# A planner that may give copies, casts and scalings to either of two engines, with other step order and buffer limits

## The chip, the core and the metric

The kernel runs on one core of one Trainium2 chip. A core has a matrix engine (TensorE, "PE" in the profile, with its weight loads as "PEld"), a vector engine (VectorE, DVE), a scalar engine (ScalarE, ACT), GpSimd (POOL) and SyncE (SP). Each engine works through its own queue of instructions in order. In this kernel SP issues nearly all DMAs, POOL issues the DMAs that add into a buffer, and the engines wait for each other through semaphores. The metric is the device time of one execution in microseconds, as the median of several runs.

## The reference, cut to what matters

The reference computes two layers of a decoder over 512 positions of width 1024, in float32. Each layer is a mixer, a gated feed-forward part with a short causal convolution, and a gated embedding part, each between two RMS norms:

```python
for i in range(DEPTH):                                   # DEPTH = 2
    h = rmsnorm(x, mix_pre_g[i]);  z = h @ w_in[i]       # 1024 x 3206
    out_a = spatial_gating(gelu(a_u), gelu(a_v), ...)    # 4 heads x 64
    out_b = silu(r_g) * norm(retention_chunkwise(rq, rk, rv))   # 6 heads x 64, rotary
    out_c = forgetting_attention(f_q, f_k, f_v, log_f)   # 6 heads x 64, softmax
    x = x + rmsnorm(concatenate([out_a, out_b, out_c]) @ w_o[i], mix_post_g[i])
    h = rmsnorm(x, ffn_pre_g[i])
    g = causal_conv3(h @ w_gate[i]) + conv_b[i]          # 1024 x 4096
    x = x + rmsnorm((gelu(g) * (h @ w_up[i])) @ w_down[i], ffn_post_g[i])
    gate = sigmoid(rmsnorm(x, ple_pre_g[i]) @ w_ple_gate[i])
    x = x + rmsnorm((p[i] @ w_ple_proj[i]) * gate, ple_post_g[i])
```

## The kernel before, in words

**Arithmetic.** A float32 product is made of three matmuls in the faster type `fp32r`: each operand is held as a rounded high part and the remainder, and high x high, high x low and low x high are summed (`mm3`). The helper `split` makes the two parts: a copy into an `fp32r` tile (the high part, a CAST on ACT in the version before) and a subtraction on DVE (the low part, a TENSOR_TENSOR). Every weight that arrives by DMA (`graw`, `traw`, `eraw`) passes through `split`. The gate and up projections are computed in pairs by a seven-product scheme (`seven`): sums of weights are formed (`wg`, `wsa`, `wsb`, `wu`: by adding DMAs from POOL and additions on DVE, `seven_weights`), and the products accumulate in three PSUM banks, `beta`, `alpha` and `gamma`. Between the products the running value of `beta` is copied out twice (`gs`), that of `gamma` once (`us`), and the final `beta` is scaled into `us`. Since PE goes on adding into the same bank, it must wait at each of these copies until the copy has read the bank; another bank's product of 12 matmuls lies between.

**Stages of a layer.** The mixer steps stand in the string `STEPS`: `u`, `v`, `F` and `H` are projections and sums, `f0` to `f2` and `r0` to `r2` are the seven-product projections of the attention and the retention pairs, `a0` to `a2` the attention itself (`fox_attend`: scores `sps`, exponential `pe`, division by its sum, transposes `tps`, copies `fet`), `c0` to `c2` the retention, `g`, `G`, `L`, `s` the gates. Then come the output product (`wo`), the embedding product (`eps`), the feed-forward part, and the gated embedding part. In the feed-forward part 32 blocks of gate and up projections run; from block 4 on each also carries a quarter of the down products (`dn`) of the blocks before it.

**What sets the order.** The program records all instructions first (class `Plan`, `record`) and then plans (`issue`): it goes through time with its own costs (`cost`, `HOP`), puts each instruction whose inputs are there on its engine, earliest recorded first, and thereby fixes each engine's queue. The queues are then in order on the chip. Buffers are taken while planning: `AHEAD` says, by kind of work ("mix", "wo", "dn" for the down weights and so on), how many recorded instructions ahead of the oldest unfinished one a buffer may be taken, and `SETS` says how many large buffers lie in each of two regions, X and W. All instructions are issued by one line, so that the profile shows nearly all under L452 (L480 in the changed kernel); rows are told apart by their tiles.

Of the kernel before, what the change touches and what calls it, by code (L numbers as in the profile page):

```python
# [36 lines left out]
P = 128  # L37
# [13 lines left out]
class Plan:  # L51
# [95 lines left out]

    @staticmethod
# [21 lines left out]
    def record(self, engine, fn, method, args, kw):  # L170
# [36 lines left out]
        self.ops.append((engine, fn, args, kw, deps, used, self.cost(engine, method, outs, ins, args, kw)))  # L207
# [44 lines left out]
    def issue(self):  # L252
        ops = self.ops
# [67 lines left out]
        def take(i, now):  # L321
# [13 lines left out]
            heapq.heappush(waiting[o[0]], (at, i, i))  # L335
# [57 lines left out]
        columns = {}  # L393
        now = 0.0
        while len(order) < n:
            progress = False
            for e in names:
                while waiting[e] and waiting[e][0][0] <= now:
                    _, pr, i = heapq.heappop(waiting[e])
                    heapq.heappush(ready[e], (pr, i))  # L400
                if ready[e] and free[e] <= now:
# [37 lines left out]
            for e in names:  # L439
                if ready[e]:  # L440
# [53 lines left out]
STEPS = "u F H f0 g f1 r0 a0 v a1 G L s r1 r2 c0 f2 c1 c2 a2"  # L494
# [37 lines left out]
def body(ctx, tc, a, out):  # L532
# [3 lines left out]
        ("DVE", nc.vector), ("ACT", nc.scalar), ("POOL", nc.gpsimd), ("PE", nc.tensor), ("SP", nc.sync)))  # L536

# [110 lines left out]
    def split(dst_hi, dst_lo, src):  # L648
        A.copy(dst_hi, src)
# [45 lines left out]
    class Mixed(Plain):  # L695
# [11 lines left out]
        def __call__(self, c, x, halves=range(2)):  # L707
# [9 lines left out]
            for kh in halves:  # L717
# [6 lines left out]
                A.copy(self.whole[kh][:, :, ts], ps)  # L724
# [135 lines left out]
    def seven(h, ws, gs, us, scale=1.0, between=None):  # L860
# [13 lines left out]
        A.copy(gs[:, t1], be)  # L874
# [3 lines left out]
        A.copy(gs[:, t2], be)  # L878
        product(ga, part(sa, 1), "hd", True, False)
        if scale == 1.0:  # L880
            A.copy(us[:, t2], ga)
        else:
            A.mul(us[:, t2], ga, -scale)
# [9 lines left out]
        A.mul(us[:, t1], be, -scale)  # L893
# [47 lines left out]
    def mixers(l, hT, uv, ready):  # L941
# [28 lines left out]
        def ret_values():  # L970
            tm_chunk_major(hT, tm_units(a["w_rv"][l], 384), 384, lambda c, ps: (V.tensor_copy if c % 2 else A.copy)(rv[:, c, :], ps[:, 0:384]))
# [42 lines left out]
        def fox_values():  # L1014
# [4 lines left out]
            def fv_done(c, ps):  # L1019
                A.copy(fv[:, c, :], ps[:, 0:384])  # L1020
# [45 lines left out]
        def fox_attend(p, tiles):  # L1066
# [4 lines left out]
            for c in range(NCH):  # L1071
# [5 lines left out]
                for s, ps in enumerate(pss):  # L1077
# [10 lines left out]
                    V.tensor_scalar(out=e[:, 0:n], in0=e[:, 0:n], scalar1=den, scalar2=None, op0=ALU.mult)  # L1088
# [3 lines left out]
                    (A.copy if c % 2 else V.tensor_copy)(et[s][:, 0:c + 1, c, :], tp[:, 0:n].rearrange("p (j t) -> p j t", t=P))  # L1092
# [11 lines left out]
        def ret_gate():  # L1104
            ps = bank("gps")
            fm_mm(ps, hT, fm_units(a["w_rg"][l]))
            A.copy(sg[:, 2, :], ps)
# [426 lines left out]
```

## Time and profile before

| | |
|---|---|
| median of 3 runs | 1566.68 us (1566.16 to 1568.85) |
| profiled execution, own time | 1566.79 us |
| its span, first to last instruction | 1564.8 us |
| PE busy | 1546.8 us |
| DVE busy | 1219.5 us |
| ACT busy | 888.6 us |
| POOL busy | 193.3 us |
| granted PE clock over the span | 0.998 |
| DMA | 239.00 MB, mean 153 GB/s |

The recorded duration of a matmul overlaps with the next one's, so a busy PE may still lose a little time between two matmuls; a wait is seen as idle time only as far as it is longer than that overlap. The durations on DVE and ACT overlap with the next instruction's too, by a smaller amount. "Idle before, releaser" is the time in which the engine stood still just before the instruction, and what ended it.

### The profile page before, as it was taken

The page shows a single profiled execution, that of the slowest core. Times are in us where ns is not written, and L with a number is a line of the kernel's source. Part 1 is how long each engine was busy: PE and PEld are TensorE (multiplying, and loading weights), DVE is VectorE, ACT ScalarE, POOL GpSimd, SP SyncE. Part 2 cuts the span into 40 slices and gives each one's busy share as a digit, 9 for nine tenths or more (in the row PEclk, how much of TensorE's full clock was granted, in tenths as well). Part 3 has the DMA queues.
Part 4 walks back from the last instruction along what each step waited for, and adds up shares of the span by engine and source line. Part 5 has one row for each costly group of instructions (what it writes and reads, how often), then busy time and mean ns, then how long its engine had stood idle before and what let it go on. Part 6 is the DMA issues. An engine that isn't in the chain of part 4 may idle for free.

```text
span 1564.8 us, 26898 instructions
## 1 busy us (share of the span) xinstructions
PE 1546.8 (99%) x10554; PEld 1401.3 (90%) x10554; DVE 1219.5 (78%) x2036; ACT 888.6 (57%) x1501; POOL 193.3 (12%) x233
## 2 busy tenths in 40 slices
PE   9999999999999999999999999999999999999997
PEld 6998878999899999998889898799999999999986
DVE  6778978977778778767796789799677788687685
ACT  8556647765554545535584576586555455455362
POOL 1111112101101111000120101121101011011010
PEclk9999999999999999999999999999999999999999
DMA  9444529545637446456474346295546455455641
GB/s 331 92 123 104 180 90 291 134 121 142 169 81 198 137 96 176 130 156 247 155 216 102 85 122 210 76 301 136 145 112 155 143 136 147 128 150 148 232 158 54
DMA packets 87877, 239.00 MB, mean 153 GB/s; under 512 B 10036, under 2 KB 18364, under 8 KB 87752
## 3 DMA queue, kind: packets, MB, share of 16 engines
q1 hardware_dynamic: 64856, 195.81, 36.0%
q0 software_dynamic: 22464, 40.90, 16.4%
q8 instruction: 82, 1.34, 0.3%
q10 hardware_dynamic: 432, 0.59, 0.1%
q14 instruction: 43, 0.35, 0.1%
HBM read 219.94 MB, written 17.33 MB: 152 GB/s over the span
## 4 chain that ended last, share of the span: by engine, by line
PE 91%; ACT 3%; DMA 3%; DVE 2%; issue 1%; SPq 0%; POOLq 0%; POOL 0%; DVEq 0%; ACTq 0%
PE beta L452 26%; PE dn L452 21%; PE ps L452 14%; PE gamma L452 13%; PE alpha L452 6%; PE wo L452 3%; DMA graw<-in_w_gu_dram 2%; PE hps L452 1%; PE sps L452 1%; PE tps L452 1%; PE ops L452 1%; PE eps L452 1%; PE gps L452 1%; ACT thl L452 1%; PE rops L452 1%
## 5 line engine op out<-in xcount | busy, mean ns | idle before, releaser
L452 PE MATMUL dn<-thl,act 128*128 128x512 f32 x1536 | 370.5, 391 | 0.0
L452 PEld LDWEIGHTS dn<-thl,act 128*128 128x128 f32 x1536 | 280.4, 188 | 52.3
L452 PE MATMUL ps<-thl,hT 128*128 128x512 f32 (+3 forms) x984 | 209.7, 368 | 1.1 <-ACT hT L452 0.9
L452 POOL DMA_DIRECT2D graw<-in_w_gu_dram x128 | 112.4, 917 | 759.0 <-DVE wg L452 162.2
L452 PEld LDWEIGHTS ps<-thl,hT 128*128 128x128 f32 x984 | 175.1, 188 | 25.0 <-ACT hT L452 1.5
L452 DVE TENSOR_TENSOR thl<-traw,thl 128x1024 fp32r<-128x1024 f32 (+3 forms) x124 | 142.3, 1155 | 19.3 <-ACT thl L452 19.2
L452 ACT CAST thl<-traw 128x1024 fp32r<-128x1024 f32 (+3 forms) x124 | 121.3, 995 | 22.0 <-DVE wsb L452 8.9
L452 PEld LDWEIGHTS beta<-hh,wu 128*128 128x128 f32 x936 | 125.6, 188 | 9.1
L452 PE MATMUL beta<-hh,wu 128*128 128x256 f32 x936 | 130.2, 279 | 0.0
L452 PE MATMUL beta<-hh,wsa 128*128 128x256 f32 x936 | 122.0, 279 | 1.2 <-ACT gs L452 0.8
L452 PE MATMUL beta<-hh,wsb 128*128 128x256 f32 x936 | 120.5, 278 | 2.0 <-ACT gs L452 1.5
L452 PE MATMUL gamma<-hhd,wsa 128*128 128x256 f32 x936 | 121.7, 278 | 0.0
L452 DVE TENSOR_TENSOR wsb<-graw,wsb 128x1024 fp32r<-128x1024 f32 x78 | 95.3, 1222 | 29.5 <-PE beta L452 16.8
L452 PEld LDWEIGHTS beta<-hh,wsa 128*128 128x128 f32 x936 | 113.4, 188 | 2.6 <-ACT gs L452 1.4
L452 PEld LDWEIGHTS beta<-hh,wsb 128*128 128x128 f32 x936 | 112.9, 188 | 2.8 <-ACT gs L452 2.1
L452 DVE TENSOR_TENSOR graw<-graw 128x512 f32<-128x512 f32 x156 | 106.3, 686 | 10.8 <-DMA graw<-in_w_gu_dram 8.3
L452 PEld LDWEIGHTS gamma<-hhd,wsa 128*128 128x128 f32 x936 | 113.8, 188 | 0.0
L452 DVE TENSOR_TENSOR facc<-dn,facc 128x512 f32<-128x512 f32 x112 | 77.0, 687 | 45.1 <-PE dn L452 44.8
L452 DVE TENSOR_TENSOR wg<-graw,wg 128x1024 fp32r<-128x1024 f32 x78 | 95.2, 1220 | 15.8 <-ACT wg L452 8.7
L452 DVE TENSOR_TENSOR wsa<-graw,wsa 128x1024 fp32r<-128x1024 f32 x78 | 95.2, 1220 | 14.7 <-ACT wsa L452 14.6
L452 PE MATMUL beta<-hb,wg 128*128 128x256 f32 x768 | 100.5, 278 | 1.3 <-DVE hb L452 0.8
L452 DVE SCALAR_TENSOR_TENSOR cv<-gs,cw,cv 128x511 f32<-128x511 f32 (+1 forms) x128 | 95.3, 745 | 7.5 <-ACT cv L452 7.1
(225 smaller groups left out, 2625.4 us busy)
## 6 DMA issues: line engine op xcount, KB each, us to landing
graw<-in_w_gu_dram SPq DMA_DIRECT2D x128, 512.0 KB
graw<-in_w_gu_dram POOLq DMA_DIRECT2D x128, 256.0 KB, 5.4
traw<-in_w_dn_dram SPq DMA_DIRECT2D x64, 512.0 KB
x<-x SPq DMA_DIRECT2D x40, 512.0 KB
graw<-in_w_fm_dram SPq DMA_DIRECT2D x28, 512.0 KB
traw<-in_w_wo_dram SPq DMA_DIRECT2D x16, 512.0 KB
traw<-in_w_pg_dram SPq DMA_DIRECT2D x16, 512.0 KB
graw<-in_w_fm_dram POOLq DMA_DIRECT2D x28, 256.0 KB, 4.7
```

What stands on the lines that cost most here:

```text
L452: made = o[1](*[self.map(v) for v in o[2]], **{k: self.map(v) for k, v in o[3].items()})
```

## The change

`plan.either` gives a third kind of engine, `E`. What is recorded there carries two forms, one for ACT (`copy`, `mul`) and one for DVE (`tensor_copy`, `tensor_scalar`), each with its planned cost. When its inputs are there it stands in both engines' lists, and whichever takes it first keeps it. The high part in `split`, the copies of `beta` and `gamma` in `seven`, the copies `rv`, `fv`, `e`, `facc`, `hw` and `sg`, the division in `fox_attend` (DVE before) and the copies `fet` (alternating by hand before) go there. `STEPS`, `AHEAD` and `SETS` have other values. The work of PE, its number of instructions and the DMAs are the same in kind and number.

```diff
-    SETS = {"X": 17, "W": 7}
-    AHEAD = {"mix": 416, "wo": 450, "wo2": 381, "emb": 503, "gu0": 443, "gu": 478, "dn": 673, "end": 164, "pg": 300, "pg2": 392}
+    SETS = {"X": 15, "W": 9}
+    AHEAD = {"mix": 411, "wo": 680, "wo2": 345, "emb": 279, "gu0": 332, "gu": 467, "dn": 1857, "end": 151, "pg": 295, "pg2": 510}
...
+            def copy(self, out, in_):
+                plan.record("ANY", {"ACT": (act.copy, (out, in_), {}, "copy"), "DVE": (vec.tensor_copy, (out, in_), {}, "tensor_copy")}, "copy", (out, in_), {})
...
-            heapq.heappush(waiting[o[0]], (at, i, i))
+            for e in ("ACT", "DVE") if o[0] == "ANY" else (o[0],):
+                heapq.heappush(waiting[e], (at, i, i))
...
+                    if ops[i][0] == "ANY":
+                        begun.add(i)
+                        fn, args, kw, cost = ops[i][1][e]
+                        ops[i] = (e, fn, args, kw, *ops[i][4:6], cost)
...
-STEPS = "u F H f0 g f1 r0 a0 v a1 G L s r1 r2 c0 f2 c1 c2 a2"
+STEPS = "u F H f0 g r0 f1 a0 v a1 r2 G s r1 L c0 f2 c1 c2 a2"
...
     def split(dst_hi, dst_lo, src):
-        A.copy(dst_hi, src)
+        E.copy(dst_hi, src)
...
         product(be, part(wg, 0), "b11", True, False)
-        A.copy(gs[:, t1], be)
+        E.copy(gs[:, t1], be)
...
         product(be, part(sa, 0), "h6", False, False)
-        A.copy(gs[:, t2], be)
+        E.copy(gs[:, t2], be)
...
-            A.copy(us[:, t2], ga)
+            E.copy(us[:, t2], ga)
...
-                    V.tensor_scalar(out=e[:, 0:n], in0=e[:, 0:n], scalar1=den, scalar2=None, op0=ALU.mult)
+                    E.mul(e[:, 0:n], e[:, 0:n], den[:, 0:1])
...
-                    (A.copy if c % 2 else V.tensor_copy)(et[s][:, 0:c + 1, c, :], tp[:, 0:n].rearrange("p (j t) -> p j t", t=P))
+                    E.copy(et[s][:, 0:c + 1, c, :], tp[:, 0:n].rearrange("p (j t) -> p j t", t=P))
```

Of the instructions that moved, these are the largest kinds, counted over each program: of 128 `gs` copies ACT keeps 70 and DVE takes 58; of 64 `us` copies from `gamma` 39 and 25; of 64 scalings of `beta` into `us` 57 and 7; of 78 `wsb` casts 48 and 30; of 78 `wu` casts 62 and 16; of 48 divisions of `pe`, all on DVE before, ACT takes 29. In all ACT has 1224 instructions instead of 1385 and DVE 2199 instead of 2038.

Three places show what this does to the queues. The first is the start of the program, where `e` is an embedding product copied out of PSUM (`eps`), `thl` a split weight, `h`, `hps` and `hT` the normalised input, its transpose in PSUM and the split of that. ACT before:

```order
L452 COPY e<-eps 128x512
L452 CAST pT<-pps 128x256 x2
L452 ACTIVATE junk,ss<-x 128x512
L452 COPY e<-eps 128x512
L452 CAST thl<-traw 128x512 x2
L452 COPY e<-eps 128x512
L452 CAST thl<-traw 128x512 x2
L452 COPY e<-eps 128x512
L452 CAST hT<-hps 128x4x128
```

ACT now, at the same place:

```order
L480 CAST pT<-pps 128x256 x2
L480 ACTIVATE junk,ss<-x 128x512
L480 CAST thl<-traw 128x512 x5
L480 COPY e<-eps 128x512
L480 CAST hT<-hps 128x4x128
```

Three of the four `e` copies went to DVE, where they now stand among the subtractions, ahead of `h`:

```order
L480 COPY e<-eps 128x512
L480 TENSOR_TENSOR thl<-traw,thl 128x512
L480 TENSOR_TENSOR pT<-pps,pT 128x256 x2
L480 COPY e<-eps 128x512
L480 SCALAR_TENSOR_TENSOR vh<-ss 128x1
L480 TENSOR_TENSOR thl<-traw,thl 128x512
L480 COPY e<-eps 128x512
L480 SCALAR_TENSOR_TENSOR h<-x,rs,gain 128x512
```

The second place is the first attention of layer 0 (`a0`). DVE before; `rm` and `rr` are the rotation of the retention pair that runs at the same time, and `rr` comes from ACT:

```order
L452 TENSOR_TENSOR rm<-rm,rr 128x512
L452 TENSOR_SCALAR pe<-pe,den 128x128 x2
L452 ISA pe,nm<-sps,fcb 128x128
L452 ISA nm 128x1
L452 ISA pe,nm<-sps,fcb 128x384
L452 ISA nm 128x1
L452 TENSOR_TENSOR rm<-rm,mix_201 128x512
L452 TENSOR_TENSOR rr<-rr,mix_168 128x512
L452 COPY fet<-tps 128x128
L452 TENSOR_TENSOR rm<-rm,rr 128x512
L452 COPY fet<-tps 128x128
```

DVE now, up to the first `fet` copy:

```order
L480 TENSOR_TENSOR thl<-traw,thl 128x2x384
L480 SCALAR_TENSOR_TENSOR fqk<-beta,fqk 128x256
L480 RECIPROCAL den<-den 128x1 x2
L480 TENSOR_TENSOR thl<-traw,thl 128x2x384
L480 TENSOR_TENSOR fqk<-gamma,fqk 128x256
L480 TENSOR_TENSOR thl<-traw,thl 128x2x384
L480 TENSOR_SCALAR fqk<-beta 128x256
L480 COPY fet<-tps 128x128
```

The division of `pe` and the other early `fet` copies stand on ACT now, and the rotation has gone from here, since `r0` comes earlier in `STEPS`.

The third place is the feed-forward part of layer 0, at the end of block 11 and the beginning of block 12 (blocks counted from 0). ACT before; `thl` is a split down weight, and the first `gs` copy is that of `beta` after the first product of the block:

```order
L452 ACTIVATE cv<-cv 128x512
L452 CAST thl<-traw 128x1024
L452 ACTIVATE us<-beta 128x256
L452 CAST thl<-traw 128x1024
L452 COPY gs<-beta 128x256
L452 CAST act<-cv 128x512
L452 CAST wsa<-graw 128x1024
L452 CAST wu<-graw 128x512
L452 COPY gs<-beta 128x256
```

ACT now, at the same place:

```order
L480 CAST thl<-traw 128x1024 x2
L480 ACTIVATE cv<-cv 128x512
L480 ACTIVATE us<-beta 128x256
L480 CAST act<-cv 128x512
L480 CAST thl<-traw 128x1024
L480 CAST wg<-graw 128x1024
L480 COPY gs<-beta 128x256
```

DVE now, at the same place:

```order
L480 TENSOR_TENSOR thl<-traw,thl 128x1024 x2
L480 TENSOR_TENSOR facc<-dn,facc 128x512
L480 TENSOR_TENSOR cv<-cv,us 128x512
L480 COPY gs<-beta 128x256
L480 TENSOR_TENSOR act<-cv,act 128x512
L480 TENSOR_TENSOR gs<-alpha,gs 128x256
L480 TENSOR_TENSOR thl<-traw,thl 128x1024
L480 TENSOR_TENSOR wg<-graw,wg 128x1024
L480 COPY us<-gamma 128x256
```

The first `gs` copy no longer stands behind a `thl` cast on ACT; it stands on DVE behind the product `cv<-cv,us`. One `thl` cast is left at the beginning of block 12, with a `wg` cast and the block's second `gs` copy behind it; this order recurs in every fourth block (12, 16, 20, 24, 28).

More of the change, by code (lines that the diff above doesn't have):

```diff
@@ L146, in engine, with either, mul @@
         return Engine()
+    def either(self, act, vec):
+        plan = self
+        class Either:
+            def copy(self, out, in_):
+                plan.record("ANY", {"ACT": (act.copy, (out, in_), {}, "copy"), "DVE": (vec.tensor_copy, (out, in_), {}, "tensor_copy")}, "copy", (out, in_), {})
+            def mul(self, out, in_, by):
+                kw = {"out": out, "in0": in_, "scalar1": by, "scalar2": None, "op0": ALU.mult}
+                plan.record("ANY", {"ACT": (act.mul, (out, in_, by), {}, "mul"), "DVE": (vec.tensor_scalar, (), kw, "tensor_scalar")}, "mul", (out, in_, by), {})
+        return Either()
     @staticmethod
@@ L392, in issue @@
                 offer(i, 0.0)
-        columns = {}
+        columns, begun = {}, set()
         now = 0.0
@@ L439, in issue @@
             for e in names:
+                while ready[e] and ready[e][0][1] in begun:
+                    heapq.heappop(ready[e])
+                while waiting[e] and waiting[e][0][2] in begun:
+                    heapq.heappop(waiting[e])
                 if ready[e]:
```

29 lines of the change are left out of this document (18 added, 11 removed).

## The prediction, made before the changed kernel was run

> **What bounds the kernel now.** I read the page first, then the waits of PE, then the chain in order of time, then the places themselves. The page's first part and its chain of work that ended last:
>
> ```profile
> span 1564.8 us, 26898 instructions
> PE 1546.8 (99%) x10554; PEld 1401.3 (90%) x10554; DVE 1219.5 (78%) x2036; ACT 888.6 (57%) x1501; POOL 193.3 (12%) x233
> ...
> PE 91%; ACT 3%; DMA 3%; DVE 2%; issue 1%; SPq 0%; POOLq 0%; POOL 0%; DVEq 0%; ACTq 0%
> ```
>
> PE is the bound, and its work is the same after the change. ACT and DVE matter only where PE waits for them. PE's waits, with the total, the number of times and the longest in us:
>
> ```profile
> PE beta L452 <- ACT gs L452: 2.4, 5, 0.6
> PE idle L452 <- POOL idle L452: 1.5, 1, 1.5
> PE hps L452 <- DVE h L452: 1.3, 3, 0.5
> PE tps L452 <- DVE fet L452: 1.1, 1, 1.1
> PE ps L452 <- ACT hT L452: 0.9, 1, 0.9
> PE beta L452 <- DVE hb L452: 0.8, 1, 0.8
> PE beta L452 <- ACT fqk L452: 0.7, 2, 0.5
> ```
>
> The second row is the program's first matmul and stays. The other six are 7.2 us in 13 waits. They are understated, as these rows of the groups by form and of the chain (start, us, what) show:
>
> ```profile
> L452 PE MATMUL dn<-thl,act 128*128 128x512 f32 x1536 | 370.5, 391 | 0.0
> ```
>
> ```profile
> 301.29 7.35 DMA graw<-in_w_gu_dram
> 333.25 5.01 PE dn L452 x22
> 339.09 2.38 PE beta L452 x21
> 408.91 8.45 DMA graw<-in_w_gu_dram
> 534.54 7.09 DMA traw<-in_w_dn_dram
> 859.53 2.83 PE beta L452 x24
> 1179.55 7.97 DMA graw<-in_w_gu_dram
> ```
>
> 22 `dn` matmuls take 5.01 us, 228 ns each, but each is recorded with 391 ns, so a wait shows only beyond some 0.16 us. With that the 13 waits are 7.2 + 13 x 0.16 = 9.3 us. This is about all that a better assignment can win: 0.6% of the span. The four DMA pieces are the places in the feed-forward parts where a weight came late and the lateness reached PE; between them PE runs at its pace.
>
> **The change, part by part.**
>
> *Balance.* The prices by form:
>
> ```profile
> L452 ACT COPY gs<-beta 128x256 f32<-128x256 f32 x128 | 47.3, 370 | 28.6 <-PE beta L452 28.0
> L452 ACT CAST wsb<-graw 128x1024 fp32r<-128x1024 f32 x78 | 82.0, 1051 | 26.9 <-PE gamma L452 15.7 <-PE alpha L452 8.8 <-DVE graw L452 2.1
> L452 DVE COPY fet<-tps 128x384 f32<-128x384 f32 x12 | 6.6, 554 | 1.5 <-PE tps L452 1.4
> L452 DVE COPY fet<-tps 128x128 f32<-128x128 f32 x12 | 3.4, 283 | 0.0
> L452 DVE TENSOR_SCALAR pe<-pe,den 128x512 f32<-128x512 f32 x12 | 5.3, 482 | 0.0
> L452 DVE TENSOR_TENSOR wsb<-graw,wsb 128x1024 fp32r<-128x1024 f32 x78 | 95.3, 1222 | 29.5 <-PE beta L452 16.8 <-ACT wsb L452 12.6
> ```
>
> A copy of 256 elements out of PSUM on DVE lies midway between 128 and 384: (283 + 554) / 2 = 418 ns, against ACT's 370. A cast of 1024 elements from SBUF on DVE is not in the trace. It is bounded by 0.48 us (the one-source row of 512 elements) and 1.22 us (the two-source row of 1024); I take twice the one-source row, 0.96 us. The largest kinds then take 58 x 0.37 + 25 x 0.37 + 30 x 1.05 = 62 us from ACT and give DVE (58 + 25) x 0.42 + 30 x 0.96 = 64 us (49 to 71 by the bounds). DVE comes to about 1280 of 1565 us, 82%. Its share is not the bound at either price, so I cost the balance at nothing; what hides it is PE's own work. What counts is the order at the waits.
>
> *The start* (term 1). ACT and PE, then PE nine us later:
>
> ```profile
> 15.56 0.61 ACT L452 COPY e<-eps 128x512 f32<-128x512 f32 x1
> 16.04 0.62 ACT L452 CAST hT<-hps 128x512 fp32r<-128x512 f32 x1
> 16.71 0.73 PE L452 MATMUL ps<-thl,hT 128*128 128x512 f32 x2 [0.91 <-ACT hT L452]
> ...
> 24.55 0.66 PE L452 MATMUL hps<-k_ident,h 128*128 128x128 f32 x4 [0.45 <-DVE h L452]
> ```
>
> PE waits for `hT`, which stands on ACT behind the fourth `e` copy, and later for `h`, whose norms ACT squares late. Three `e` copies, 0.6 us each, leave ACT; the fourth still stands directly before `hT`, and five `thl` casts now come ahead of it. So the first wait shrinks little and the second should go, since ACT reaches the squares earlier. Ceiling (0.91 + 0.16) + (0.45 + 0.16) = 1.7 us; against it, one `e` copy more ahead of `h` on DVE is 0.6 us. I take -0.8 (between +0.6 and -1.7).
>
> *The first attention* (term 2). DVE, then PE:
>
> ```profile
> 108.47 0.69 DVE L452 TENSOR_TENSOR rm<-rm,mix 128x512 f32<-128x512 f32 x1 [1.58 <-ACT rr L452]
> ...
> 110.02 0.33 PE L452 MATMUL tps<-k_ident,pe 128*128 128x128 f32 x1 [1.14 <-DVE fet L452]
> ```
>
> DVE stood 1.58 us waiting for `rr` from ACT, with the `fet` copy queued two additions behind it, and PE stood for `fet`. `r0` now comes earlier, and only one of the two early `fet` copies is on DVE, behind split subtractions that wait for an ACT cast at most. I take -1.0 of 1.14 + 0.16 = 1.3 us (0 to -1.3).
>
> *The feed-forward parts* (term 3). SP, ACT and PE at the third place of the orders:
>
> ```profile
> 408.65 0.80 SPq L452 DMA_DIRECT2D traw<-in_w_dn_dram  x2
> ...
> 413.62 1.05 ACT L452 CAST thl<-traw 128x1024 fp32r<-128x1024 f32 x1 [1.29 <-DMA traw<-in_w_dn_dram]
> ...
> 417.21 1.05 ACT L452 CAST thl<-traw 128x1024 fp32r<-128x1024 f32 x1 [1.32 <-DMA traw<-in_w_dn_dram]
> ...
> 418.17 0.36 ACT L452 COPY gs<-beta 128x256 f32<-128x256 f32 x1
> ...
> 418.58 1.68 PE L452 MATMUL beta<-hh,wsa 128*128 128x256 f32 x12 [0.39 <-ACT gs L452]
> ...
> 422.27 1.63 PE L452 MATMUL beta<-hh,wsb 128*128 128x256 f32 x12 [0.59 <-ACT gs L452]
> ```
>
> ACT waits for a down weight (1.29 and 1.32 us), the `gs` copy stands behind the cast, and PE stops twice. The changed program mends both causes here. This `gs` copy is on DVE. And with the limit for "dn" at 1857 the loads are released earlier: counted in PE's work between the matmul that frees the load's buffer and the last one that ACT's queue waits for ahead of the cast, the first six down loads of layer 0 had 23.5, 23.5, 13.8, 16.6, 2.7 and 9.5 us (matmuls at 228 and 113 ns) and now have 22.6, 22.6, 43.1, 52.7, 26.2 and 35.4. I credit these two waits (0.39 + 0.59 + 0.32 = 1.3) and the one behind the `traw` piece at 534.54, at the mean of the five, 2.4 / 5 + 0.16 = 0.6: -1.9. The pieces at 301.29 and 1179.55 are `graw`, whose loads are not released earlier, and stay. Ends: 0 and -(2.4 + 5 x 0.16) = -3.2.
>
> *Other waits* (term 4). `fqk`, 0.7 + 0.32 = 1.0 us, is an eviction in the mixers that has two engines now; I take half, -0.5 (0 to -1.0). `hb` stays on ACT in both and the two later `hps` waits have the same chain ahead: 0.
>
> *New waits* (term 5). 83 evictions of `beta` and `gamma` stand on DVE among subtractions of 1.22 us, where none stood. On ACT 5 of 128 `gs` copies cost PE 0.64 us each; at that rate 83 x 5/128 x 0.64 = 2.1 us. DVE gets a copy only where the plan sees it free first, so I take +0.8 (0 to +2.1).
>
> Sum: -0.8 - 1.0 - 1.9 - 0.5 + 0.8 = -3.4 us. The profiled execution took 1566.79, 0.1 above the median of 1566.68 and 2.0 above its span; from the median this gives **1563.3 us**, with 1559.5 (all lower ends, -7.2) to 1569.4 (all upper ends, +2.7).
>
> **The rivals.**
>
> *The waits only change places: 1566.3.* The same costs made both plans, and waits arise where the chip departs from the costs; another plan departs elsewhere. Against it: terms 2 and 3 name a queue order that is gone. Half of term 5's upper end more, and terms 1 and 4 at zero, give -3.4 + 1.3 + 1.1 + 0.6 = -0.4.
>
> *A late down weight recurs: 1574, slower.* In blocks 12, 16, 20, 24 and 28 of each layer one `thl` cast on ACT now has only 2.7 us of PE's work between release and cast, and behind it `wg` and the second `gs` copy. PE needs that copy 48 matmuls after the block's start, 2.7 + 48 x 0.113 = 8.1 us after the release. Cast, cast and copy take 1.05 + 1.05 + 0.37, and a hop some 0.2 us: the load must land within 5.4 us. It did at 408.65 (cast at 413.62, 5.0 us), and did not in the piece at 534.54 (7.1). At 6.5 us each of the 10 places costs 1.1: +11. Against it: no `graw` load is issued shortly ahead of these loads now, as was the case at 534.54.
>
> *The port between DVE and POOL: 1570, slower.* POOL's adding DMAs and DVE's one-source operations in SBUF, at the two places of the trace where they met, here the first:
>
> ```profile
> 130.04 0.86 POOL L452 DMA_DIRECT2D graw<-in_w_fm_dram  x1 [3.05 <-PE sps L452]
> 130.22 0.51 DVE L452 TENSOR_SCALAR pe<-pe,den 128x256 f32<-128x256 f32 x1
> ...
> L452 POOL DMA_DIRECT2D graw<-in_w_gu_dram x128 | 112.4, 917 | 759.0 <-DVE wg L452 162.2
> ```
>
> The issue took 0.86 us, not more than the mean of 0.92, so nothing was held. Were it held, some 70 DVE casts and 156 issues would meet 70 x 156 x (0.96 + 0.92) / 1565 = 13 times; at 0.96 us each and half of them reaching PE that is +6.2 on the forecast. The Trainium skill ("SBUF — State Buffer", section "SBUF: two separate sides") states this rule: a DVE copy of fp32 within SBUF locks GpSimd out of a shared port, and a DMA issued from GpSimd cannot have its descriptors written meanwhile. By that rule the change would lose; the trace does not agree at the place shown.
>
> *More than the waits: 1558.* 24 matmuls of 256 columns take 2.83 us in one stretch (118 ns) and 21 take 2.38 in another (113). A mixer order that avoids the slower pace could win 2 us beyond the lower ends; nothing in the order aims at it.
>
> **How the numbers follow.** Forecast 0.50, waits change places 0.26, late down weight 0.13, port 0.05, more than the waits 0.06. A measurement of this kernel can tell 0.2%, 3.1 us, from no change. Faster: 0.40 of the forecast and 0.06, together 0.46. Same: 0.10 of the forecast and 0.22 of the first rival, 0.32. Slower: 0.04 of the first rival, 0.13 and 0.05, 0.22. The range reaches from 1557 to 1572: it takes in the ends of the sum, the port and the low case, and leaves out most of the late down weight. The forecast's own range is 1559.5 to 1566.
>
> **What would show it.** Right: PE's waits for `gs` at two or three instead of five and mostly behind `graw`; none for `fet` of 1 us; none for `h` before 30 us; no wait of ACT for `traw` in the feed-forward parts beyond half a us. Wrong: PE waits for DVE `gs` or `us` (term 5); PE waits for ACT `gs` at equal distances of some 60 us, ACT's `thl` waiting for `traw` just before (the late down weight); POOL issues longer than 1.2 us beside DVE casts (the port).

## The result: 1.4% slower, and the profile after

The changed kernel takes 1589.23 us as the median of its runs (1586.78 to 1592.21) against 1566.68 before, 1.0142 times as long, with a 95% interval of 1.0128 to 1.0156. The forecast was 1563.3 us, with a range of 1557 to 1572. The profiled execution has a span of 1587.5 us, 22.7 more than before. The page's first part and its chain of the work that ended last:

```profile
span 1587.5 us, 26948 instructions
PE 1552.8 (98%) x10554; PEld 1404.2 (88%) x10554; DVE 1290.9 (81%) x2197; ACT 814.0 (51%) x1340; POOL 191.0 (12%) x233
...
PE 67%; DMA 16%; DVE 12%; issue 2%; ACT 2%; POOL 0%; SPq 0%; POOLq 0%; DVEq 0%; ACTq 0%
```

The busy times came out nearly as forecast (DVE at 81% where 82% stood in the text), and PE is still the busiest engine. But DMA has 16% of the chain instead of 3, and DVE 12 instead of 2. PE's waits, with the total, the number of times and the longest in us:

```profile
PE beta L480 <- DVE gs L480: 11.9, 13, 1.7
PE beta L480 <- ACT fqk L480: 2.8, 1, 2.8
PE ps L480 <- ACT hT L480: 1.5, 2, 0.9
PE beta L480 <- ACT wsa L480: 1.5, 2, 0.9
...
PE beta L480 <- DVE fqk L480: 0.9, 2, 0.4
PE beta L480 <- ACT gs L480: 0.8, 1, 0.8
```

All of PE's waits, without the first matmul's 1.5, come to 24.9 us in 35 against 7.9 in 16 before (the prediction's 7.2 in 13 leave out three short rows). With the 0.16 us that a row hides of each wait, the difference is 17.0 + 19 x 0.16 = 20.0 of the 22.7 us. So the time went into PE's waits, some 14 us of it, with the hidden part, into one row: `gs` on DVE. The row `fet` is gone, and `gs` on ACT has one wait instead of five.

Most of the rest goes with PE's clock. In this row of a stretch of 5 us behind the wait for `fqk` (its length; busy us of PE, PEld, DVE, ACT and POOL with their instructions; then the granted clock as a share of the full one, the DMA share and GB/s) PE ran at 0.66:

```profile
72.00:77.00 5.00, 5.00 (x32) 5.00 (x31) 3.88 (x13) 0.61 (x1) 0.00 (x0) 0.66 0.05 9
```

From 18 to 22 us, behind two waits for `hT`, it was 0.57. That is 0.34 x 5 + 0.43 x 4 = 3.4 us of PE's work; in the kernel before no stretch in which PE had work shows such a clock. Waits and clock together are 23.4 us, a little more than the 22.7 by which the span grew.

Where the DVE row comes from is seen at one of its places. First the chain of waits of the changed kernel (start, us, what), then the two additions on DVE there (start, us, the instruction, and in brackets the idle time before it):

```profile
455.21 6.63 DMA graw<-in_w_gu_dram
...
463.20 8.00 DMA graw<-in_w_gu_dram
...
471.23 0.70 DVE graw L480
...
472.65 0.60 DVE facc L480
473.25 0.34 DVE wu L480
473.58 0.60 DVE cv L480
474.19 0.60 DVE graw L480
474.79 0.35 DVE gs L480
...
475.18 1.65 PE beta L480 x12
```

```profile
471.23 1.42 DVE L480 TENSOR_TENSOR graw<-graw 128x512 f32<-128x512 f32 x2 [2.39 <-DMA graw<-in_w_gu_dram]
```

An SP load of gate and up weights (6.63 us) is followed by POOL's adding DMA into the same buffer (8.00 us). The two additions `graw<-graw` at the head of DVE's queue wait for that DMA, and DVE stands still for 2.39 us. The `gs` copy is queued behind them, behind `facc`, `wu`, `cv` and one more addition, and PE stands until it is done. No weight itself is late for PE here: the copy is late because it stands in the same queue. In the steady feed-forward parts DVE's wait comes back every second block (about 31 us), and 11 of PE's 13 waits for `gs` on DVE, 10.5 us, stand behind one of these. DVE's waits for these sums in the kernel before and in the changed one:

```profile
DVE graw L452 <- DMA graw<-in_w_gu_dram: 8.3, 7, 2.2
```

```profile
DVE graw L480 <- DMA graw<-in_w_gu_dram: 41.4, 21, 2.7
```

And SP's issue of four such loads, in one stretch of each kernel:

```profile
474.46 2.54 SPq L452 DMA_DIRECT2D graw<-in_w_gu_dram  x4
```

```profile
455.21 9.96 SPq L480 DMA_DIRECT2D graw<-in_w_gu_dram  x4
```

In the changed kernel SP stands between the first pair and the second for some 9 us, since the second waits for a buffer (its releaser is the last `gamma<-hb,wsb` matmul); its transfer then runs beside the adding DMA. Before, both pairs went out together here (not everywhere: at 444.42 and 469.60 us two pairs went out apart). That the loads themselves now come later for their use shows on ACT, whose casts of `wu` wait for them, before and in the changed kernel:

```profile
ACT wu L452 <- DMA graw<-in_w_gu_dram: 1.1, 3, 0.8
```

```profile
ACT wu L480 <- DMA graw<-in_w_gu_dram: 34.5, 27, 4.0
```

The adding DMAs are not slower on the whole: from issue to landing they take 5.2 us in the median, 5.4 before.

### The profile page after: what moved, and what is told of

Same layout as the page of the kernel before. It is cut to its first block, busy times and chain, and to the rows that moved or that the text cites. A ratio compares the mean times of both kernels' runs of the same rounds, so it can differ in the third digit from the quotient of the medians.

```text
span 1587.5 us, 26948 instructions
## 1 busy us (share of the span) xinstructions
PE 1552.8 (98%) x10554; PEld 1404.2 (88%) x10554; DVE 1290.9 (81%) x2197; ACT 814.0 (51%) x1340; POOL 191.0 (12%) x233
## 4 chain that ended last, share of the span: by engine, by line
PE 67%; DMA 16%; DVE 12%; issue 2%; ACT 2%; POOL 0%; SPq 0%; POOLq 0%; DVEq 0%; ACTq 0%
PE beta L480 17%; DMA graw<-in_w_gu_dram 14%; PE ps L480 14%; PE dn L480 14%; PE gamma L480 9%; PE alpha L480 3%; PE wo L480 2%; DVE graw L480 2%; DVE cv L480 1%; PE hps L480 1%; DVE thl L480 1%; PE eps L480 1%; PE sps L480 1%; DVE wsb L480 1%; PE ops L480 1%
## 5 line engine op out<-in xcount | busy, mean ns | idle before, releaser
L480 DVE TENSOR_TENSOR graw<-graw 128x512 f32<-128x512 f32 x156 | 106.5, 685 | 42.9 <-DMA graw<-in_w_gu_dram 41.4
L480 PE MATMUL beta<-hh,wsa 128*128 128x256 f32 x936 | 125.2, 281 | 15.5 <-DVE gs L480 11.9
L480 ACT CAST thl<-traw 128x1024 fp32r<-128x1024 f32 (+3 forms) x113 | 110.0, 993 | 17.6 <-DVE wsb L480 14.6
L480 ACT CAST wsa<-graw 128x1024 fp32r<-128x1024 f32 x76 | 79.8, 1049 | 58.5 <-DVE wsb L480 37.1
L480 PE MATMUL alpha<-hb,wg 128*128 128x256 f32 x768 | 98.7, 277 | 0.0
L480 PE MATMUL gamma<-hb,wsb 128*128 128x256 f32 x768 | 98.3, 277 | 0.0
```

Of the source, the lines that this page charges most:

```text
L480: made = o[1](*[self.map(v) for v in o[2]], **{k: self.map(v) for k, v in o[3].items()})
```

## The experiments

They separate six theories. **1**: copies that PE waits for stand in a queue behind work on a weight that lands late. **2**: DVE simply has too much work. **3**: the new limits make weights late, whatever engine does the copies; **4** puts this on `SETS`, **5** on `AHEAD`. **6**: any new plan of this kernel loses, and the plan before is one that happens to lose little. The ratios are to the kernel before, each measured beside it on the same chip.

| version | edit | median, us | ratio | 95% interval |
|---|---|---|---|---|
| the change | | 1589.23 | 1.0142 | 1.0128 to 1.0156 |
| gs_first | the change, sums behind the copy | 1576.81 | 1.0067 | 1.0050 to 1.0085 |
| both_first | the same and casts on ACT | 1578.86 | 1.0070 | 1.0053 to 1.0087 |
| gs_act | the change, gs fixed on ACT | 1602.31 | 1.0239 | 1.0208 to 1.0271 |
| sets_old | the change, old SETS | 1582.09 | 1.0100 | 1.0085 to 1.0115 |
| lat | the change, slower landings planned | 1594.14 | 1.0174 | 1.0158 to 1.0189 |
| nudge_after | the change, 5 ns in the planner | 1593.20 | 1.0168 | 1.0146 to 1.0190 |
| t_only | before, new tables | 1583.89 | 1.0110 | 1.0095 to 1.0125 |
| ahead_only | before, new AHEAD | 1575.78 | 1.0054 | 1.0040 to 1.0067 |
| sets_only | before, new SETS | 1571.84 | 1.0030 | 1.0017 to 1.0043 |
| e_only | before, free choice | 1581.94 | 1.0099 | 1.0080 to 1.0118 |
| e_evict | before, free choice of evictions | 1582.54 | 1.0095 | 1.0080 to 1.0110 |
| e_split | before, free choice of casts | 1577.87 | 1.0066 | 1.0050 to 1.0081 |
| e_att | before, free choice in attention | 1567.98 | 1.0003 | 0.9995 to 1.0012 |
| lat_before | before, slower landings planned | 1577.96 | 1.0072 | 1.0055 to 1.0089 |
| copy_first2 | before, gs ahead of casts on ACT | 1569.46 | 1.0014 | 1.0005 to 1.0023 |
| nudge_dve | before, 5 ns in the planner | 1571.30 | 1.0025 | 1.0013 to 1.0036 |
| nudge_act | before, 5 ns in the planner | 1568.06 | 1.0009 | 1.0000 to 1.0018 |

### The sums behind the copy

The edit acts on the finished order of DVE; `copies` are the numbers of the `gs` copies, `adds` those of the additions `graw<-graw`:

```diff
...
+        for q, i in enumerate(line):
+            if i in self.copies:
+                for j in reversed(line[max(0, q - 6):q]):
+                    if j in self.adds and j not in moved and all(u in moved or place[u] > place[i] for u in users[j]):
+                        moved.add(j)
+                        later.setdefault(i, []).insert(0, j)
+        order = [x for i in order if i not in moved for x in (i, *later.get(i, ()))]
...
```

> The changed program with one edit behind the planner: where up to six places ahead of a gs copy on DVE there stand additions graw<-graw (which wait for POOL's adding DMAs), they are put right behind that copy. PE's, ACT's, SP's and POOL's queues are the same word for word. Theory 1 (the gs copies wait behind additions whose weights are late): PE's waits for gs on DVE, 11.9 us in 13 in the changed kernel, fall below 2 us, and the time falls by 10 to 16 us, to 1573 to 1579. Theory 2 (DVE has too much work at these places, whatever the order): what the copies win is lost at the weights that the additions make, PE waits for wsa instead of gs, and the time stays within 4 us of 1589.

1576.81 us: 0.75% of the 1.42 is gone, about 12 us. The same two rows in this version:

```profile
PE beta L491 <- DVE gs L491: 4.3, 9, 1.0
...
DVE graw L491 <- DMA graw<-in_w_gu_dram: 8.7, 7, 2.5
```

Theory 1 holds for this part: the queues of PE, ACT, POOL and SP are the same, DVE does the same work, and only the order of two kinds of instruction on it differs. DVE's waiting for these sums falls from 41.4 to 8.7 us, since they have mostly landed by the time DVE gets to them. The waits for `gs` fell less far than I had put down (4.3, not below 2): 0.5 us in the mean, most of them in every fourth block. That the time still fell as far as I had said is in part luck: of the 14.5 us between the two profiled spans PE's waits explain 8.5 (24.9 us in 35 against 17.0 in 31, with 0.16 each), and the 3.4 us of low clock, absent here, are the next largest part. Of these, the 1.7 us at the start can't be owed to the edit, since this version has the same waits for `hT` there (1.5 us in two on ACT, 0.6 on DVE).

### The copies fixed on ACT

```diff
-        E.copy(gs[:, t1], be)
+        A.copy(gs[:, t1], be)
...
-        E.copy(gs[:, t2], be)
+        A.copy(gs[:, t2], be)
```

> The changed kernel with only the two gs copies of each block fixed on ACT again; the planner plans all else anew. Theory 1: PE's waits for gs are back at 2 to 4 us, DVE's waits for late sums stay above 25 us, and what is left of the loss is at the start and in the first mixer: 1572 to 1578. Theory 3: 1583 or more, with PE waiting for weights.

1602.31 us, the slowest version of all. The figures put down for theory 1 are missed altogether. The time is in theory 3's range (1583 or more), and PE does wait more for weights (`wsa`, 7.2 us in 5 instead of 2.3 in 3), but this is not the largest row. PE waits as long for `gs` on ACT as it did on DVE, and the chain of waits shows why:

```profile
PE beta L480 <- ACT gs L480: 12.3, 11, 2.4
...
463.50 8.46 DMA graw<-in_w_gu_dram
...
471.99 0.70 DVE graw L480
...
474.34 0.61 DVE cv L480
...
474.97 0.05 ACT act L480
...
475.50 0.37 ACT gs L480
```

The late sum holds DVE as before; DVE's `cv` comes late, ACT's `act<-cv` waits for it, and the copy is queued behind `act` on ACT. A copy on the other engine is no safer while one instruction ahead of it there depends on the queue that stands still. So what counts is where the waiting sums stand in DVE's queue, not which engine has the copy. What else this version loses is in good part PE's clock, which was 0.51 from 294 to 301 us, 0.58 from 946 to 950, 0.57 from 1082 to 1090 and 0.57 from 1386 to 1390, each time behind waits of 2.0 to 2.4 us: 9 us of PE's work, against 3.4 in the changed kernel. A new row is `oa` on DVE in the mixers, 3.6 us.

### The tables without the free choice

The version t_only is the kernel before with the three lines of the change at `SETS`, `AHEAD` and `STEPS`, and nothing else.

> The kernel before with the new STEPS, AHEAD and SETS alone; every copy stays on the engine it had. Theory 1: DVE still waits long for late sums (over 25 us in all), but the gs copies stand on ACT, so PE hardly waits for them: 1565 to 1573. Theory 3 (the new limits make the weights themselves late, and whoever makes them holds PE): 1580 or more, with PE's waits at wsa, wsb or gs on ACT.

1583.89 us: +1.1% with every copy on its old engine. PE's largest wait, and the chain at one of its places:

```profile
PE beta L452 <- ACT gs L452: 11.0, 15, 2.4
...
460.98 6.37 DMA graw<-in_w_gu_dram
...
467.37 0.63 ACT wu L452
...
468.02 0.69 DVE wu L452
...
469.31 0.61 DVE cv L452
...
470.47 0.38 ACT gs L452
```

It is the same pattern with another weight: the second pair of loads, issued 9 us after the first, lands at 467.3; the cast `wu` on ACT and its subtraction on DVE wait for it, `cv` stands behind these, `act` waits for `cv`, and `gs` stands behind `act`. Theory 1 in the form that I had (it takes a copy on DVE behind a late sum) falls; theory 3 holds for the lateness, and the path from a late weight to the copy exists on both engines.

### The free choice without the tables

The version e_only is the changed kernel with the old three lines.

> The changed kernel with the old STEPS, AHEAD and SETS: only the free choice between ACT and DVE. Theory 1: it takes both a late weight and a copy behind it. With the old limits DVE waits for late sums some 8 us in all, as before the change, so few copies are caught: 1566 to 1574. Theory 2 (DVE's load): the same casts and copies are on DVE, so 1582 or more.

1581.94 us, again not what theory 1 gave. With the old tables the steady feed-forward parts are nearly clean (PE waits 1.2 us between 320 and 780 us, 7.3 in the changed kernel), and PE's list has no wait for `gs` at all. So copies on DVE do not bring this wait by themselves, while the tables bring it without them (11.0 us in t_only). The loss here is at the first feed-forward blocks. The windows of 32 us there, before and in this version (the figures as in the row of the clock above), and PE's waits of this version:

```profile
280.00:312.00 32.00, 32.00 (x251) 30.89 (x250) 30.90 (x44) 23.38 (x38) 6.16 (x8) 1.00 0.61 149
```

```profile
280.00:312.00 32.00, 24.63 (x196) 23.94 (x195) 32.00 (x48) 20.25 (x31) 4.41 (x5) 0.89 0.59 146
...
PE beta L480 <- ACT wsa L480: 6.4, 2, 5.8
...
PE beta L480 <- ACT fqk L480: 2.3, 1, 2.3
```

DVE was busy for 30.90 of 32 us here before the change already, and for all 32 now, while ACT is down to 20.25 and PE stands for 5.8 us and, after two matmuls, for 1.6 more; behind that its granted clock was 0.57 from 304 to 312 us, another 2 us. The chain that ends in these waits runs on DVE alone from 284 to 308 us. Theory 2 holds at this place: over the span DVE has a fifth of its time free, but in these blocks it had none to give. The second cause is the mixer's `fqk`, taken up below.

### Casts, evictions and attention apart

Each is the kernel before with the new kind of engine for one group alone: `split`; or `gs`, `us`, `e`, `hw`, `rv`, `fv`, `sg` and `facc`; or the division and `fet`.

```diff
-        A.copy(dst_hi, src)
+        E.copy(dst_hi, src)
```

> The kernel before with the free choice for the high parts in split alone (the casts of weights and activations); evictions and attention stay on their engines. If the casts on DVE are what makes the first feed-forward blocks late (wsa waits 5.8 us in the version with the whole free choice), this costs 8 to 15 us: 1575 to 1582. If it is the evictions in DVE's queue, within 4 us of before.

> The kernel before with the free choice for the evictions alone (gs, us, e, hw, rv, fv, sg, facc); the casts in split stay on ACT. If DVE's subtractions are pushed back by evictions, so that POOL's adding DMAs and the sums come late: 8 to 15 us slower, 1575 to 1582. If it is the casts, within 4 us of before.

> The kernel before with the free choice in the attention alone (the division of pe and the fet copies). By the row of the first attention, where PE waits 1.14 us for fet, this wins 1 us and loses nothing else: 1565 to 1567. If the planner's new order of the mixers meets other waits: 1569 to 1573.

Casts alone cost 0.66%, evictions alone 0.95%, and both together (with attention) 0.99%: the two do not add, and neither alone explains the 5.8 us at the first blocks. With evictions alone PE waits most behind `wsa` (3.7 us) and behind one `gs` on DVE (2.8 us) which stood behind a gate and up transfer that took 9.42 us; with casts alone behind `h` (2.9 us in 9), `wsa` (2.9 us, in layer 1) and `gs` on ACT (2.8). The attention alone makes no difference that can be measured, where I had put down 1 us less. PE's wait for `fet` is gone there too, but waits for `h` rise from 1.3 to 2.1 us.

### AHEAD, SETS and the planner's landing times

> The kernel before with the new AHEAD alone. If AHEAD makes up what SETS (+5 us) leaves of the tables' 17 us: 8 to 14 us slower, 1575 to 1581. If the parts only lose together (the limits were fitted to each other and to STEPS): 1566 to 1573.

> The kernel before with SETS alone at 15 and 9. Theory 4: 8 to 14 us slower than before, 1575 to 1581, with the stalls in the feed-forward parts behind late gate and up weights. Theory 5: within 4 us of before, 1563 to 1571.

> The changed kernel with SETS alone back at 17 buffers in X and 7 in W. In the changed kernel one of each two gate and up loads waits for a buffer that the last wsb product of the same block frees, and lands only just ahead of its use. Theory 4 (the new SETS leaves these loads the late buffer): PE's stalls in the steady feed-forward parts, 15.9 us in the changed kernel against 3.2 before, fall below 7 us, and the time by 8 to 14 us, to 1575 to 1581. Theory 5 (the new limits in AHEAD do it): within 4 us of 1589.

`AHEAD` alone costs 0.54%, spread over the mixers and the first blocks; `SETS` alone 0.30%, its largest wait being four of `gs` in the feed-forward part of layer 0 (4.0 us); the two are 0.84% of the tables' 1.10, and `STEPS` alone was not tried. Giving the changed kernel its old `SETS` back wins 0.42%, and PE's waits for `gs` on DVE fall from 11.9 us to 4.6. So in the changed kernel theory 4 has the right place, at half of the size that I expected. In the kernel before theory 5 has the larger share, but 0.30% for `SETS` is hardly more than the 0.25% that a plan changed without an aim costs (below).

```diff
-                        rate, wait = (215.0, 4500) if e == "POOL" else (340.0, 2600)
+                        rate, wait = (215.0, 6500) if e == "POOL" else (340.0, 4000)
```

> The changed kernel, with the planner told other landing times: 6.5 us instead of 4.5 behind the transfer for POOL's adding DMAs, 4.0 instead of 2.6 for SP's loads, as the slower ones of the profile land (POOL's median is 4.7 us from the issue, its slowest tenth 8.1). If the loss comes from DVE's and ACT's queues being planned for landings that come later on the chip (theory 1), the additions move behind the copies in the plan, PE's waits for gs fall to 2 to 5 us and the time to 1572 to 1579. If the lateness lies in the buffers and no order could hide it (theory 4 alone), 1583 or more.

> The kernel before with the same two landing times in the planner and nothing else. By theory 1 a plan with the slow landings has no copy queued behind a late weight: 2 to 4 us less than before, 1562 to 1565. Against it: the old tables were set with the old landing times, and another plan may lose as much elsewhere: 1567 to 1580.

With the longer landing times the planner puts the sums behind the copies by itself. In the version lat PE waits 1.2 us between 320 and 780 us and not at all between 1090 and 1500, where the changed kernel has 7.3 and 5.4. That bears out theory 1's cause at these places: the queues were planned for a landing of 5.7 us after the issue (256 KB at 215 GB/s and 4.5 us), and the adding DMA took 8.00. Which of the two landing times does it was not tried apart. But the kernel is slower on the whole, at 1594.14 us and not the 1572 to 1579 that I had put down for theory 1, since the first blocks of both layers lose more, some 5 us of it to a low clock behind the waits (0.54 from 298 to 309 us, 0.57 from 1083 to 1087):

```profile
PE beta L480 <- ACT wsa L480: 10.5, 3, 6.6
```

For the kernel before the same figures cost 0.72%. A planner with truer numbers at one place is not a better planner for the whole.

### A change that aims at nothing

```diff
-    HOP = {"PE": 197, "DVE": 128, "ACT": 131, "POOL": 80, "SP": 0}
+    HOP = {"PE": 197, "DVE": 133, "ACT": 131, "POOL": 80, "SP": 0}
```

The version nudge_act has 136 for ACT instead.

> The kernel before, where the planner reckons 133 ns instead of 128 from the end of a DVE instruction to its followers. Nothing is aimed at; the plan only comes out another way (the queues of PE, DVE and ACT differ in a few hundred rows). Theory 6 (any new plan of this kernel meets late weights at other places, and the plan before is one that happens to meet few): 5 to 15 us slower than before, 1572 to 1582, and this much of every loss above belongs to no part of the change. Against it: within 3 us of before, and the losses above belong to the edits.

> The kernel before with 136 ns instead of 131 for ACT in the planner. Theory 6: 5 to 15 us slower than before, 1572 to 1582, not by the same amount as with DVE's figure. Against it: within 3 us of before.

> The changed kernel with 133 ns instead of 128 for DVE in the planner. In the feed-forward parts the loads have the same distances to their uses as in the changed kernel. Theories 1 and 4: the recurring waits for gs stay, 1583 to 1595. Theory 6 alone: anywhere from 1570 to 1600, with the feed-forward waits gone or elsewhere.

A plan changed this little costs 0.25% and 0.09%: in this form theory 6 accounts for 1 to 4 us, not for 15 to 22. A wider form is not shut out. Plans that differ by more than a nudge lose more even where no copy changes its engine (lat_before 0.72%, ahead_only 0.54%), so that part of each loss can be that of a plan to which the old tables were not fitted; that these tables were fitted to the old plan is itself not shown. In the version nudge_after PE's waits for `gs` on DVE stand mostly 31 us apart too (14.6 us in 15), so the recurring pattern does not hang on one lucky or unlucky plan.

### The copies first, on ACT too

In copy_first2, in the kernel before, casts of `thl` and `wu` directly ahead of a `gs` copy on ACT are put behind it, by a loop like the one above (up to three places ahead, as long as one such cast follows another).

> The kernel before with one edit behind the planner: where casts of freshly landed weights (thl, wu) stand on ACT right ahead of a gs copy, they are put right behind it (some 20 places; PE's, DVE's, POOL's and SP's queues stay word for word). Theory 1 says that the wait of PE for gs on ACT, 2.4 us in 5, comes from these: it falls to 1 us or less at the two places behind thl and in part at the two behind wu, and the time falls by 1 to 2.5 us, to 1564.5 to 1566. If casts that come later hold PE at the weights instead: 1567 to 1570.

> The version gs_first, and on ACT too the casts of wg and wu that stand up to four places ahead of a gs or fqk copy are put right behind it (some 20 places, the fqk copy of the first mixer at 68 us among them). If the 2.8 us wait for fqk comes from the cast of wu that waits 3.02 us for its load, with wg behind it, the wait falls below 1.5 us (the table load of 1.28 us still stands ahead of the copy) and the time by 1 to 3 us against gs_first, to 1574 to 1576. If the waits only move to the weights: 1576 to 1580.

In copy_first2 the row of `gs` falls from 2.4 us in 5 to 0.4 in 1, and the time is 0.14% longer. What came instead is the next copy in the block:

```profile
PE gamma L464 <- ACT us L464: 2.2, 2, 1.4
```

In both_first the wait for `fqk` goes the way that was expected. ACT in the changed kernel, then in this version:

```profile
68.29 0.62 ACT L480 CAST wu<-graw 128x512 fp32r<-128x512 f32 x1 [3.02 <-DMA graw<-in_w_fm_dram]
...
70.35 1.03 ACT L480 CAST wg<-graw 128x1024 fp32r<-128x1024 f32 x1
71.28 0.36 ACT L480 COPY fqk<-beta 128x256 f32<-128x256 f32 x1
```

```profile
66.92 0.37 ACT L499 COPY fqk<-beta 128x256 f32<-128x256 f32 x1 [0.81 <-PE beta L499]
...
PE gamma L499 <- DVE us L499: 2.8, 10, 0.3
```

The copy runs as soon as PE is through with its product, and PE's wait there, 2.8 us in the changed kernel and 1.8 in gs_first, is gone, with one of 0.4 for the next `fqk` left. Theory 1 is shown for this wait as well. Yet the time is the same as that of gs_first: ten short waits for `us` on DVE have come, in every fourth block, where a cast of `wg` was moved behind a copy. No version tried is faster than the kernel before.

## Why the prediction was wrong, point by point

**The bound** was read rightly: PE, without gaps, and at most some 9 us to win. That very reading says that nearly any new wait counts in full, with little to set against it; the sum treated new waits as the smallest of its terms.

**Term 5, the new waits, is the step that failed**, and with it the premise of term 3 that the gate and up loads "are not released earlier, and stay". Term 5 put down +0.8 us (0 to +2.1) against 11.9 us in 13 waits, 14.0 with what the rows hide. It was sized by the rate at which copies on ACT had cost PE, 5 of 128, and by "DVE gets a copy only where the plan sees it free first". Both take the chip to be free where the plan is. On DVE the copies stand behind additions that wait for a DMA, with a landing that the plan reckons at 5.7 us and that took 8.00 in the case shown. The right price is the wait of the instruction ahead of the copy, not the copy's own. And the row does not come from the new engine: with the old tables it is missing (e_only) or 2.8 us in one wait (e_evict), with the new ones and the old engines it is 11.0 us on ACT (t_only). The lateness of the gate and up loads, which the tables brought, was costed at nothing.

**Term 3** read one of its two places only in part. Of PE's wait of 0.59 us at 422.27 the prediction says that it comes from the cast of a late down weight. The chain before the change (start, us, what), from the landing of the 8.45 us `graw` piece that the prediction shows and passes over:

```profile
417.39 0.04 DVE graw L452
...
419.13 0.70 DVE cv L452
...
419.86 0.02 ACT act L452
...
421.85 0.38 ACT gs L452
```

It is the path of gs_act: POOL's adding DMA is late, DVE's sum waits for it (2.21 us there), `cv` stands behind the sum and the split of the down weight, ACT's `act` waits for `cv`, and `gs` stands behind `act`. The down weight was late too, so that mending it alone could not win this wait: in the changed kernel the one wait left for `gs` on ACT, 0.80 us at 415.38, has the same path from an adding DMA of 8.96 us. The waits for `gs` at 312.50 and 1192.41 before the change also run back to such a DMA, the pieces at 301.29 and 1179.55. So three of the five waits from which term 5 took its rate already had the pattern that the change made common. Of the waits behind `thl`, those for `gs` on ACT went from 2.4 us in 5 to 0.8 in 1, and ACT has no wait for `traw` in the feed-forward parts any more. But the distances from release to use were counted for the down loads alone. Half of the gate and up loads are released later, to judge by the SP rows (9.96 us for four instead of 2.54) and ACT's waits for them (34.5 us for `wu` instead of 1.1), and the `SETS` versions bear it out in part.

**The balance**, costed at nothing. The price was too high, and still the conclusion wrong. The rows of the changed kernel:

```profile
L480 DVE CAST wsb<-graw 128x1024 fp32r<-128x1024 f32 x30 | 20.6, 686 | 2.2 <-PE gamma L480 1.6 <-PE alpha L480 0.6
L480 DVE COPY gs<-beta 128x256 f32<-128x256 f32 x58 | 24.3, 419 | 6.2 <-PE beta L480 6.1
L480 DVE COPY e<-eps 128x512 f32<-128x512 f32 x7 | 4.8, 682 | 0.8 <-PE eps L480 0.8
```

The cast takes 0.69 us, not 0.96 (the copy out of PSUM, 0.42, came out as reckoned). A cast of 1024 elements from SBUF takes as long as a copy of 512 from PSUM. The Trainium skill ("VectorE: DVE Perf Modes", section "What auto-detection actually checks") has a rule that fits: one source and the destination in SBUF let the engine use a double-rate mode. The trace agrees. What was missed is that 82% is a mean: in the window from 280 to 312 us DVE stood at 30.90 of 32 us before the change, and there the moved work lay on the path, as e_only shows. (In the changed kernel itself the waits for `wsa` there are 2.3 us.)

**Term 1**, the start: -0.8 forecast, but the waits for `hT` rose from 0.9 to 1.5 us on ACT and 0.6 on DVE. The copies `hw`, which the change gives to either engine as well, now stand ahead of `hT` casts on both; the prediction followed `e` and not `hw`. **Term 2**: the wait for `fet`, 1.1 us, is gone as forecast, but new waits for `pe` and `nm` on DVE later in the attention, 1.1 us in all, took it back. **Term 4**: -0.5 forecast for `fqk`, +3.0 measured (0.7 to 2.8 + 0.9), by the cast of a late `wu` ahead of it.

**The rivals.** That waits only change places (1566.3) is what copy_first2, both_first and the nudges did, at its size; the change itself is far beyond it. The late down weight (1574) had the right pattern, a copy behind a weight's work at equal distances in the feed-forward parts, with the wrong weight: ACT does not wait for `traw`, DVE waits for the sums of `graw`, every second block instead of every fourth. In the sum of the first rival, 1.3 + 1.1 + 0.6, the 0.6 has no source that the text names. The port: POOL's issues take as long as before (0.92 us in the mean, both times). Here one with a DVE cast inside it:

```profile
1217.23 0.88 POOL L480 DMA_DIRECT2D graw<-in_w_gu_dram  x1 [5.50 <-PE beta L480]
...
1217.31 0.41 DVE L480 CAST wu<-graw 128x512 fp32r<-128x512 f32 x1
```

The cast took 0.41 us and the issue 0.88, neither longer than by itself. By the rule of the Trainium skill ("SBUF — State Buffer", section "SBUF: two separate sides") one of the two would have been held until the other was through; the trace shows no sign of it in these rows. But "nothing was held" in the prediction looks at the issue alone. The division in its rows took 0.51 us, and the second one that met an issue 0.40, where the ten others of that shape took 0.34 to 0.35. In the changed kernel one such division (at 890.46 us) took 0.82 us beside an operation of POOL on `sguw`. That POOL's work held DVE there is likely, but not shown: in t_only two such divisions that met an issue took their usual 0.35. At 0.5 us it would explain next to nothing of the 22.7.

**What stays open.** The parts do not add: the free choice alone costs 15 us, the tables alone 17, both together 22.6. Some 12 of these went when the sums were put behind the copy, 8.5 of them in PE's waits; the other 10 lie at the start, at `fqk`, at `wsa` in the first blocks and in the rest of the `gs` waits, and both_first shows that they do not come back one by one. Why evictions alone cost as much as the whole free choice was not settled, nor how much of each loss is that of any new plan.

## What to carry to other kernels

An in-order queue passes a wait on to everything behind it, and from there to other engines. Follow each wait of the busiest engine back along its chain to the DMA, and not only to the instruction right ahead: the chains of three of the five waits before this change already ran back to the late sums that the change made common. Before an eviction that the busiest engine waits for is moved, look at what will stand ahead of it, what that waits for (a DMA above all), and how late it has been; a share of busy time says nothing on this, and its mean over the span hides the stretches where the engine has nothing to spare. When a change alters how buffers are shared, count the distance from release to use for every kind of load, not only for the kind whose wait you saw. And where the bound engine has no gaps, a redistribution can win little and lose much: the odds of the forecast should say so.

## What was not expected

Taking one wait away by itself rarely gave its time back: the 2.0 us saved at `gs` in copy_first2 came with 2.2 us of waits for `us`, and a time 0.14% longer. Two plans that differ only by 5 ns in the planner's reckoning differ by 0.25% and 0.09% from the kernel before, so that for this kernel an effect below some 4 us can't be laid to an edit that makes the planner plan anew; the versions that only reorder one finished queue do not have this blur.

A long wait of PE costs more than its length. In the profiled executions of all versions each of the nine single waits of 2.7 us or more was followed by some microseconds at a granted clock of about a half: in the changed kernel 2.8 us for `fqk` cost 1.7 us more, and in e_only 5.8 us for `wsa` cost 2 more. Of the waits between 1.8 and 2.4 us some were followed by it and some not.
